# Row gradient of an 8192 x 8192 matrix: issuing each transfer midway through the one in front of it

**Chip, cores, metric.** One core of one Trainium2 chip. The metric is the device time of one execution in microseconds (us).

## What is computed

```python
def reference(x: np.ndarray) -> np.ndarray:      # x: 8192 x 8192, float32
    return np.gradient(x, axis=1)
```

Inside a row this is `(x[j+1] - x[j-1]) / 2`; at the two ends of a row it is the plain difference of the first two and of the last two elements. 268.4 MB are read and 268.4 MB written, with hardly any arithmetic.

## The kernel before

The matrix is cut into 32 sets. A set is a tile of 128 partitions with two rows each (64 KB on each partition, 8 MB in all). Three slots in SBUF are used in turn. GpSimd takes the differences at the row ends; VectorE makes the halved differences of both rows in one instruction and writes them, shifted by 64 elements, into the slot that it reads; the end values are then copied in, on VectorE or GpSimd, and the slot is stored. All transfers are issued by SyncE on one queue.

```python
    def load(i):
        b = slots[i % NB]
        ins = nc.sync.dma_start(out=b[:, SH : SH + W], in_=x_sets[i])
        loads.append(chain(i, ins, *([stores[i - NB]] if i >= NB else [])))
    ...
        for i in range(NB):                       # NB = 3
            load(i)
        for i in range(nsets):                    # nsets = 32
            ...                                   # GpSimd: ends
            last = i == nsets - 1
            nr = 1 if last else R                 # R = 2
            for r in range(0, R, nr):
                ...                               # VectorE: both rows at once; then the copy of the ends
                ins = nc.sync.dma_start(out=out_sets[i, :, ...], in_=b[:, ...])
                stores[i] = chain(i, ins, placed)
                if 2 <= i and not last:
                    tc.add_manual_dep(ins.ins, stores[i - 1].ins.name, landed, reason="behind a load that has begun")
            if 1 <= i and i - 1 + NB < nsets:
                load(i - 1 + NB)
```

`chain` only tells the framework which of the dependencies within a slot need a semaphore. The manual dependency makes a store wait, on the issuing side, until the store before it has landed. By then a load has begun. Store i and load i+2 so enter the queue together.

## Time and profile before

| | before |
|---|---|
| device time, first 3 runs | 1250.43 us median (1250.28 to 1250.81) |
| profiled run: span | 1247.7 us |
| DMA queue, share of 16 engines | 99.6% |
| VectorE busy | 554.8 us |
| one 8 MB transfer | 19.319 us between completions |

The last row comes from the DMA packet records, which lie in the trace beneath the page's totals: one record for each packet (here 64 KB, or 4 bytes for a completion), with its start and duration. The records don't name the engine, but each engine's packets follow one another end to end, so 16 chains can be followed. Everything below on "the last packet of a load" or on "spread" is worked out from them. Packet loss means the sum of what the packets took over 2.418 us for 64 KB, divided by 16: the time that it costs an engine on average.

The page's list of DMA issues (what goes where, how often, and the median from issue to landing) in the kernel before reads:

```profile
slot<-in_x_dram SPq DMA_DIRECT2D x32, 57.6
out_dram<-slot SPq DMA_DIRECT2D x31, 38.6
```

A store lands two transfers (38.6 us) after its issue, a load three (57.6 us): at each issue of the pair the queue holds nearly one whole transfer, then the store, then the load.

### The profile page before, as it was taken

The page shows a single profiled execution, that of the slowest core. Times are in us where ns is not written, and L with a number is a line of the kernel's source. Part 1 is how long each engine was busy: PE and PEld are TensorE (multiplying, and loading weights), DVE is VectorE, ACT ScalarE, POOL GpSimd, SP SyncE. Part 2 cuts the span into 40 slices and gives each one's busy share as a digit, 9 for nine tenths or more (in the row PEclk, how much of TensorE's full clock was granted, in tenths as well). Part 3 has the DMA queues.
Part 4 walks back from the last instruction along what each step waited for, and adds up shares of the span by engine and source line. Part 5 has one row for each costly group of instructions (what it writes and reads, how often), then busy time and mean ns, then how long its engine had stood idle before and what let it go on. Part 6 is the DMA issues. An engine that isn't in the chain of part 4 may idle for free.

```text
span 1247.7 us, 241 instructions
## 1 busy us (share of the span) xinstructions
DVE 554.8 (44%) x54; POOL 8.8 (1%) x48
## 2 busy tenths in 40 slices
DVE  2851455324553345533455334554335543355433
POOL 0000000000000000000000000000000000000000
DMA  9999999999999999999999999999999999999998
GB/s 403 437 437 424 424 429 435 435 435 431 431 437 433 427 431 433 429 435 437 437 437 435 427 431 437 427 433 437 437 437 437 435 431 429 435 433 437 431 433 357
DMA packets 9361, 536.88 MB, mean 430 GB/s; under 512 B 1040, under 2 KB 1040, under 8 KB 1040
## 3 DMA queue, kind: packets, MB, share of 16 engines
q1 hardware_dynamic: 9360, 536.88, 99.6%
q14 instruction: 1, 0.01, 0.0%
HBM read 268.44 MB, written 268.44 MB: 430 GB/s over the span
## 4 chain that ended last, share of the span: by engine, by line
another core or an unknown queue 68%; DVE 18%; DMA 8%; issue 3%; POOL 1%; POOLq 0%
DVE slot L82 18%; DMA slot<-in_x_dram 5%; DMA out_dram<-slot 3%; POOL ends L71 0%; POOL slot L93 0%; DVE slot L93 0%; POOLq L129 0%
## 5 line engine op out<-in xcount | busy, mean ns | idle before, releaser
L82 DVE CUSTOM_DVE_ANT_0 slot<-slot 128x16382 f32<-128x16382 f32 (+1 forms) x33 | 551.3, 16706 | 670.6 <-POOL ends L71 670.6
L71 POOL TENSOR_TENSOR ends<-slot 128x4 f32<-128x4 f32 x32 | 6.3, 198 | 991.5 <-DMA slot<-in_x_dram 991.5
L93 DVE COPY slot<-ends 128x4 f32<-128x4 f32 (+1 forms) x21 | 3.6, 171 | 0.7
L93 POOL COPY slot<-ends 128x4 f32<-128x4 f32 x12 | 2.3, 190 | 207.8 <-DVE slot L82 207.8
L118 POOL MEMSET const-bfloat16-1.0<- 128x1 bf16 x1 | 0.1, 102 | 0.0
L118 POOL MEMSET const-uint8-127<- 128x1 uint8 x1 | 0.1, 102 | 0.0
L118 POOL MEMSET const-float32-0.0<- 128x1 f32 x1 | 0.1, 98 | 0.2 <-issue 0.2
L118 POOL MEMSET const-float32-1.0<- 128x1 f32 x1 | 0.1, 98 | 0.0
## 6 DMA issues: line engine op xcount, KB each, us to landing
out_dram<-slot SPq DMA_DIRECT2D x2, 4096.0 KB, 20.2
slot<-in_x_dram SPq DMA_DIRECT2D x32, 57.6
out_dram<-slot SPq DMA_DIRECT2D x31, 38.6
```

Of the source, the lines that this page charges most:

```text
L71: ins = nc.gpsimd.tensor_sub(out=ends[:, i, :, :], in0=xin[:, :, 1 : m : m - 2], in1=xin[:, :, 0 : m - 1 : m - 2],)
L82: ins = nc.vector._custom_dve(dve_ops.TENSOR_TENSOR_REDUCE_SUB_MAX, out=b[:, c0:c1], in0=b[:, SH + c0 + 1 : SH + c1 + 1], in1=b[:, SH + c0 ...
L93: ins = placer.tensor_copy(out=res[:, :, 0 : m : m - 1], in_=ends[:, i, r : r + nr, :])
L118: nc = _bacc.Bacc("TRN2", target_bir_lowering=False, num_devices=1)
```

## The change

Its intent is to issue each transfer about midway through the one in front of it, and to take the moment for that from VectorE: an instruction for one row takes half a transfer's time, so its end is a clock. The first row of a set, which starts when the load has landed, gives the issue of the next load; the second row, which is made to wait until the store in front has landed, gives the issue of the set's own store. The end copies go to ScalarE, and at the start two loads are issued instead of three.

```diff
+    def follow(ins, needed, reason):
+        tc.add_manual_dep(ins.ins, needed.ins.name, landed, reason=reason)
+
-    def load(i):
+    def load(i, after=None):
         ...
+        if after:
+            follow(ins, after, "half-way through the transfer in front")
 ...
-        for i in range(NB):
-            load(i)
+        load(0)
+        load(1)
         for i in range(nsets):
 ...
-            for r in range(0, R, nr):
-                c0, c1 = r * m + 1, (r + nr) * m - 1
+            for r in range(R):
+                c0, c1 = r * m + 1, (r + 1) * m - 1
                 ins = nc.vector._custom_dve(...)
-                halved = chain(i, ins, *at)
-                ...
-                if 2 <= i and not last:
-                    tc.add_manual_dep(ins.ins, stores[i - 1].ins.name, landed, reason="behind a load that has begun")
-            if 1 <= i and i - 1 + NB < nsets:
-                load(i - 1 + NB)
+                at = chain(i, ins, at)
+                if r == 0:
+                    if i == 2:
+                        follow(ins, stores[0], "half-way through the second store")
+                    if i == 0 or 2 <= i < nsets - 1:
+                        load(2 if i == 0 else i + 1, after=at)
+                elif not last:
+                    follow(ins, loads[i + 1] if i < 2 else stores[i - 1], "half-way through the transfer in front")
+                if last:
+                    store(i, r, 1, place(nc.vector, i, r, 1, at))
+            if not last:
+                store(i, 0, R, place(nc.scalar, i, 0, R, at))
```

More of the change, by code (lines that the diff above doesn't have):

```diff
@@ L57, in chain, with store, place @@
         return ins
-    def load(i):
+    def follow(ins, needed, reason):
+        tc.add_manual_dep(ins.ins, needed.ins.name, landed, reason=reason)
+    def load(i, after=None):
         b = slots[i % NB]
         ins = nc.sync.dma_start(out=b[:, SH : SH + W], in_=x_sets[i])
+        if after:
+            follow(ins, after, "half-way through the transfer in front")
         loads.append(chain(i, ins, *([stores[i - NB]] if i >= NB else [])))
+    def store(i, r, nr, placed):
+        ins = nc.sync.dma_start(
+            out=out_sets[i, :, r * m : (r + nr) * m], in_=slots[i % NB][:, r * m : (r + nr) * m]
+        )
+        stores[i] = chain(i, ins, placed)
+    def place(engine, i, r, nr, halved):
+        res = slots[i % NB][:, r * m : (r + nr) * m].rearrange("p (t m) -> p t m", m=m)
+        to, of = res[:, :, 0 : m : m - 1], ends[:, i, r : r + nr, :]
+        ins = nc.scalar.copy(out=to, in_=of) if engine is nc.scalar else engine.tensor_copy(out=to, in_=of)
+        return chain(i, ins, halved)
     with tc.manual_schedule():
-        for i in range(NB):
-            load(i)
+        load(0)
+        load(1)
         for i in range(nsets):
             b = slots[i % NB]
+            last = i == nsets - 1
             xin = b[:, SH : SH + W].rearrange("p (t m) -> p t m", m=m)
@@ L75 @@
             )
-            at = [chain(i, ins, loads[i])]
-            last = i == nsets - 1
-            nr = 1 if last else R
-            for r in range(0, R, nr):
-                c0, c1 = r * m + 1, (r + nr) * m - 1
+            at = chain(i, ins, loads[i])
+            for r in range(R):
+                c0, c1 = r * m + 1, (r + 1) * m - 1
                 ins = nc.vector._custom_dve(
@@ L89 @@
                 )
-                halved = chain(i, ins, *at)
-                res = b[:, r * m : (r + nr) * m].rearrange("p (t m) -> p t m", m=m)
-                placer = nc.gpsimd if i % 5 in (1, 3) and not last else nc.vector
-                ins = placer.tensor_copy(out=res[:, :, 0 : m : m - 1], in_=ends[:, i, r : r + nr, :])
-                placed = chain(i, ins, halved)
-                ins = nc.sync.dma_start(
-                    out=out_sets[i, :, r * m : (r + nr) * m], in_=b[:, r * m : (r + nr) * m]
-                )
-                stores[i] = chain(i, ins, placed)
-                if 2 <= i and not last:
-                    tc.add_manual_dep(ins.ins, stores[i - 1].ins.name, landed, reason="behind a load that has begun")
-                at = [halved]
-            if 1 <= i and i - 1 + NB < nsets:
-                load(i - 1 + NB)
+                at = chain(i, ins, at)
[10 more added lines that the diff above has]
+                store(i, 0, R, place(nc.scalar, i, 0, R, at))
 _INS = ['x']
```

## The prediction

> **What bounds the kernel now.** I read the page's busy shares and DMA rows first, then the groups, then the DMA queue's own waits, then the time line around one step, and last the DMA packet records that the trace keeps under the page's totals.
>
> The page, parts 1 to 3: the only compute engine that does anything is VectorE at 44%. The DMA queue fills 99.6% of what 16 engines can give, and the GB/s row stands at 430 to 437 nearly everywhere. A kernel like this is bound by the DMA engines, and the question is only how much of their time isn't bytes at the full rate.
>
> ```profile
> span 1247.7 us, 241 instructions
> DVE 554.8 (44%) x54; POOL 8.8 (1%) x48
> ...
> GB/s 403 437 437 424 424 429 435 435 435 431 431 437 433 427 431 433 429 435 437 437 437 435 427 431 437 427 433 437 437 437 437 435 431 429 435 433 437 431 433 357
> ...
> q1 hardware_dynamic: 9360, 536.88, 99.6%
> ```
>
> The reader should notice that the dips (424, 427) lie in the first half, and that the first slice (403) and the last (357) are the ramp at both ends.
>
> The groups split by shape give the durations that the change re-uses. The one-row form already exists, in the last set:
>
> ```profile
> L82 DVE CUSTOM_DVE_ANT_0 slot<-slot 128x16382 f32<-128x16382 f32 x31 | 533.9, 17223 | 649.4 <-POOL ends L71 649.4
> L82 DVE CUSTOM_DVE_ANT_0 slot<-slot 128x8190 f32<-128x8190 f32 x2 | 17.4, 8686 | 21.2 <-POOL ends L71 21.2
> L71 POOL TENSOR_TENSOR ends<-slot 128x4 f32<-128x4 f32 x32 | 6.3, 198 | 991.5 <-DMA slot<-in_x_dram 991.5
> ```
>
> The queue's waits say that nearly all of them are a store that waits for the store before it, which is the manual dependency of this kernel. In the time line of one step, a store and the next load are issued together, 0.4 us apart, just after a store has landed, and the next pair follows 38.67 us later:
>
> ```profile
> SPq L95 <- DMA out_dram<-slot: 1082.2, 29, 38.8
> SPq L95 <- DVE slot L93: 74.7, 3, 38.2
> ```
>
> ```profile
> 918.42 0.33 SPq L95 DMA_DIRECT2D out_dram<-slot  x1
> 918.80 0.43 SPq L61 DMA_DIRECT2D slot<-in_x_dram  x1
> 937.75 0.20 POOL L71 TENSOR_TENSOR ends<-slot 128x4 f32<-128x4 f32 x1 [20.95 <-DMA slot<-in_x_dram]
> 937.98 17.22 DVE L82 CUSTOM_DVE_ANT_0 slot<-slot 128x16382 f32<-128x16382 f32 x1 [21.44 <-POOL ends L71]
> 955.24 0.17 DVE L93 COPY slot<-ends 128x4 f32<-128x4 f32 x1
> 957.09 0.33 SPq L95 DMA_DIRECT2D out_dram<-slot  x1
> ```
>
> At 918.42 the load in front has just begun (it lands at 937.75), so each pair goes into the queue a whole transfer, 19.3 us, ahead of need. Nothing starves.
>
> The packet records size what is left. A 64 KB packet takes 2.418 us when undisturbed. Packets of one engine chain end to end, and I followed the 16 chains (some 520 packets each). A transfer is 8 packets on each engine, and its completions come 19.319 us after those of the one in front; 64 of them (the two half stores count as one) make 64 x 19.319 = 1236.4 us. The first data packet starts at 1.75 us, and its first round is slowed by 0.7 us on average. The fastest engine thus ends at 1240.8 us. The slowest ends at 1246.46 us, and the span closes 1.2 us later. Those 5.6 us of spread are the only reserve. They come almost wholly from one place: the last packet of a load, when a store is next on the queue, takes 2.5 to 3.7 us in place of 2.42. From load to load or from store to load the step stays 19.32 us. The mean loss at that switch falls from 0.85 us (first store) through 0.45, 0.23, 0.30, 0.35 to nearly 0 after 800 us, while the spread of the 16 engines grows from 0.55 us to 5.64 us: once they no longer switch together, they no longer slow one another. That this is why it fades is my inference.
>
> **What the Trainium skill says.** "DMA: Bandwidth & Descriptors", section "Where 436 GB/s comes from", gives a port ceiling of 435.2 GB/s (16 ports). The trace agrees: 8,388,608 B in 19.319 us is 434.2 GB/s, so only the ends and the switches can be won. The same page, "Queues, rings and completion order": one queue has a ring on each of 16 engines, and each consumes its own in order. That fits the spread that grows and never resets, and means that a transfer issued too late would hit the fastest engine first. "SBUF — State Buffer", section "Who interferes with whom", holds that DMA doesn't contend with a compute engine. The trace agrees: while VectorE ran from 121.2 to 138.4 us the store under way kept its 19.319 us step. "ScalarE: Activation LUTs", section "What ACT_TABLE_LOAD costs", gives some 2.7 us for a table load. The kernel before runs nothing on ScalarE, so its trace shows none; one load at the start would be over long before the first copy is due near 50 us.
>
> **The change part by part.**
>
> 1. One row for each VectorE instruction: 31 x 17.22 us become 62 x 8.69 us, that is 538.8 in place of 533.9, plus 4.9 us of VectorE time. The 19 end copies of VectorE (171 ns) and the 12 of GpSimd (190 ns) move to 31 on ScalarE. VectorE stays at some 45% of the span and has slack in each step (17.4 of 38.6 us), so the path gains and loses nothing: 0 us.
>
> 2. The issue of a load: from "together with the store before it" to "after row 0 of the set that has just landed". Landing seen, subtraction, row: about 0.4 + 0.2 + 8.7 + 0.1 = 9.4 us after the previous load landed, the store in front being half done. Before the transfer in front ends, 19.3 - 9.4 = 9.9 us are left. The spread of up to 5.6 us takes its share of this for the fastest engine, and the first issue shows 1.0 us from issue (0.74) to first packet (1.75): 9.9 - 5.6 - 1.0 = 3.3 us of margin at the worst. No gap: 0 us.
>
> 3. The issue of a store: row 1 now waits for the store before it to land, then 0.8 us until seen (landed 100.49, issue 101.30 in the records before) + 8.7 + about 0.4 for the copy = 9.9 us into the load in front. Margin 9.4 - 5.6 - 1.0 = 2.8 us. 0 us.
>
> 4. The start: the third load is no longer issued at once, but after row 0 of set 0 at 22.9 + 8.7 = 31.6 us; the second load ends at 41.5. The first store comes after row 1, which waits for that load: about 41.9 + 8.7 + 0.4 = 51 us, with the third load ending at 61. Full either way: 0 us. The end is the same: load 31 lands near 1208, the two half stores are issued near 1217.5 and 1226.3, behind a store that ends near 1227.
>
> 5. What can be gained: the pair's issue no longer falls into the first two packets after a store. In the first 300 us I count 14 such packets, 60 to 360 ns too long each, 2.2 us in all over 16 engines; of the two slowest engines one has a single such packet (215 ns), the other none. A generous reading, that these also seed the later loss, makes it 1 us. The loss at the switch from load to store isn't an issue effect by its times: at 117 to 120 us nothing had been issued for 15 us. So I keep most of it: gain 0 to 2 us, and I take 1 us.
>
> Sum: 1250.4 - 1.0 = 1249.4 us.
>
> **The rivals.**
>
> First, the switch costs less because only one transfer, not two, is queued behind the load that ends. For it: the change's own intent, and that this loss is by far the largest term. Against it: the first store (0.85 us, the costliest) already had only other work behind it that was issued at about the same moment. If true, up to the whole spread goes: 1250.4 - 5.6 = 1244.8 us. The hard floor for this queue is near it.
>
> Second, the fastest engines run dry because the margin, 3 us, is eaten by a spread greater than before. Then they wait for an issue and the spread stops growing near 9 us. The slowest engine doesn't feel this, since it always has work, but switching together again might bring the loss back: some 1 to 3 us, up to 1253.
>
> Third, the change brings a stall at every step, because an issue is late for all engines. It would take 0.4 us at each of 64 transfers to make 2%, and issues come 9 us early. I see nothing in the profile for it.
>
> **Range and chances.** The point is 1249.4 us. Eight times in 10 it should lie between 1246.0 us (most of the switch loss gone) and 1252.0 us (spread somewhat worse). Faster by 2% would be below 1225.4 us, which is below the bytes at the full rate (1236.4 us), so 0.5% is left for it. Slower by 2% is above 1275.4 us and needs the third rival: 1%. Within 2%: 98.5%.
>
> **What would show it.** Queue share near 99.6% again; the load's time from issue to landing falling from 57.6 to about 38.6 - 9.4 = 29 us and the store's from 38.6 to about 29 us; 64 VectorE instructions of 8.69 us; issues on the time line some 19 us apart, each about midway between two landings. Landings still 38.64 us apart for each pair late in the run. In the packet records, the last packet of a load should still be slow at the first switches, and the spread should end between 4 and 7 us. If the spread ends below 3 us, the first rival holds and my step 5 is wrong. If gaps show between packets of the fastest engines, the second does. A time outside 1244 to 1254 would mean that I misread what sets the end.

## The result

| | before | after |
|---|---|---|
| runs | 6 | 6 |
| median, us | 1250.36 (1249.16 to 1250.81) | 1249.68 (1248.69 to 1250.33) |
| profiled run, span, us | 1247.7 | 1248.6 |

The ratio is 0.9995 with a 95% interval of 0.9982 to 1.0008: no difference that these runs could show. The profiled run of the changed kernel was its slowest, that of the kernel before one of its faster ones, so the two spans stand the wrong way round; that is chance.

The profile of the changed kernel, first its page (span, busy shares, the queue):

```profile
span 1248.6 us, 307 instructions
DVE 556.3 (45%) x66; ACT 7.4 (1%) x32; POOL 6.6 (1%) x36
...
q1 hardware_dynamic: 9360, 536.88, 99.5%
```

The groups, costliest first (busy us, mean ns of one, then idle time before them and what ended it):

```profile
L100 DVE CUSTOM_DVE_ANT_0 slot<-slot 128x8190 f32<-128x8190 f32 x64 | 556.1, 8690 | 670.5 <-POOL ends L91 341.7
L80 ACT COPY slot<-ends 128x4 f32<-128x4 f32 x31 | 6.1, 197 | 1190.5 <-DVE slot L100 1190.5
...
L80 ACT ACT_TABLE_LOAD x1 | 1.3, 1283 | 0.7 <-PEq L134 0.7
```

64 instructions of one row stand in place of 31 of two rows and two of one; their busy time rises from 551.3 to 556.1 us, and it lies in idle time.

The DMA issues and the queue's own waits show that the change did what it set out to do. A transfer now lands 1.5 transfers after its issue (29.7 us), loads and stores alike, and the queue no longer waits for a landing but for ScalarE's copy and for VectorE's row:

```profile
slot<-in_x_dram SPq DMA_DIRECT2D x32, 29.7
out_dram<-slot SPq DMA_DIRECT2D x31, 29.6
```

```profile
SPq L72 <- ACT slot L80: 591.7, 31, 19.9
SPq L66 <- DVE slot L100: 572.0, 30, 30.0
```

And the time line of one step late in the run (start, duration, engine, line, operation):

```profile
899.86 0.20 POOL L91 TENSOR_TENSOR ends<-slot 128x4 f32<-128x4 f32 x1 [38.40 <-DMA slot<-in_x_dram]
900.09 8.69 DVE L100 CUSTOM_DVE_ANT_0 slot<-slot 128x8190 f32<-128x8190 f32 x1 [10.77 <-POOL ends L91]
908.81 0.34 SPq L66 DMA_DIRECT2D slot<-in_x_dram  x1
919.28 8.69 DVE L100 CUSTOM_DVE_ANT_0 slot<-slot 128x8190 f32<-128x8190 f32 x1 [10.50 <-DMA out_dram<-slot]
928.01 0.20 ACT L80 COPY slot<-ends 128x4 f32<-128x4 f32 x1 [38.45 <-DVE slot L100]
928.23 0.33 SPq L72 DMA_DIRECT2D out_dram<-slot  x1
938.55 0.20 POOL L91 TENSOR_TENSOR ends<-slot 128x4 f32<-128x4 f32 x1 [38.49 <-DMA slot<-in_x_dram]
```

The load is issued at 908.81 and the store at 928.23, 19.4 us apart; before, they left 0.4 us apart. Yet the distance from one load's landing to the next (899.86 to 938.55 as GpSimd sees it) is 38.69 us, as it was in the kernel before. A store is issued half a transfer later than before (29.6 us ahead of its landing in place of 38.6), a load nearly one and a half transfers later (29.7 us in place of 57.6), and the landings stayed where they were.

What the packet records say of both profiled runs:

```
                                            before   after
first data packet, us                         1.75    1.75
packet loss in all, mean engine, us           4.63    4.09
  of it at the first load-to-store switch     0.83    1.03
  of it after 50 us                           3.93    3.45
fastest / slowest engine's last packet ends  1240.8 / 1246.5   1240.4 / 1247.3
```

So the same three things make up the time in both: 1236.4 us of bytes at the full rate, 4 us of start and end, and the 7 to 8 us that the slowest engine loses, nearly all of it in the packets that end a load when a store follows.

### The profile page after: what moved, and what is told of

The parts are those of the page before. It is cut to its first block, busy times and chain, and to the rows that moved or that the text cites. A ratio compares the mean times of both kernels' runs of the same rounds, so it can differ in the third digit from the quotient of the medians.

```text
span 1248.6 us, 307 instructions
## 1 busy us (share of the span) xinstructions
DVE 556.3 (45%) x66; ACT 7.4 (1%) x32; POOL 6.6 (1%) x36
## 3 DMA queue, kind: packets, MB, share of 16 engines
q1 hardware_dynamic: 9360, 536.88, 99.5%
## 4 chain that ended last, share of the span: by engine, by line
DMA 73%; DVE 22%; issue 3%; POOL 0%; SPq 0%; POOLq 0%; ACT 0%; DVEq 0%
DMA slot<-in_x_dram 70%; DVE slot L100 22%; DMA out_dram<-slot 2%; POOL ends L91 0%; SPq L66 0%; DVE slot L80 0%; POOLq L145 0%; ACT slot L80 0%; DVEq L100 0%
## 5 line engine op out<-in xcount | busy, mean ns | idle before, releaser
L100 DVE CUSTOM_DVE_ANT_0 slot<-slot 128x8190 f32<-128x8190 f32 x64 | 556.1, 8690 | 670.5 <-POOL ends L91 341.7
L80 ACT COPY slot<-ends 128x4 f32<-128x4 f32 x31 | 6.1, 197 | 1190.5 <-DVE slot L100 1190.5
L80 ACT ACT_TABLE_LOAD x1 | 1.3, 1283 | 0.7 <-PEq L134 0.7
## 6 DMA issues: line engine op xcount, KB each, us to landing
slot<-in_x_dram SPq DMA_DIRECT2D x32, 29.7
out_dram<-slot SPq DMA_DIRECT2D x31, 29.6
```

Of the source, the lines that this page charges most:

```text
L80: ins = nc.scalar.copy(out=to, in_=of) if engine is nc.scalar else engine.tensor_copy(out=to, in_=of)
L100: ins = nc.vector._custom_dve(dve_ops.TENSOR_TENSOR_REDUCE_SUB_MAX, out=b[:, c0:c1], in0=b[:, SH + c0 + 1 : SH + c1 + 1], in1=b[:, SH + c0 ...
```

## The experiments

There are two questions. The first is whether the time really doesn't depend on when a transfer is issued, or whether two effects of the change cancel. My theory: only an empty queue costs; rivals: the row-wise instructions cost and the issue times gain, or the other way round. The second is what makes the loss at the switch from load to store, the only reserve there is, and why it fades in the run. My theory (an inference in the prediction): engines that switch together slow one another, and the loss stops as they spread. Rivals: it fades with the age of the run; it depends on issue times.

All twelve kernels gave correct results. The table has the times; ratios are against the kernel before in the same rounds on the same chip.

```
run                            median (range), us              ratio [95% interval]
e1 row-wise alone              1250.71 (1249.07 to 1251.55)    1.0003 [0.9989, 1.0017]
e2 no manual wait              1249.49 (1248.92 to 1251.72)    0.9998 [0.9984, 1.0012]
e3 issue 7.6 us later          1323.54 (1321.26 to 1327.53)    1.0591 [1.0572, 1.0610]
e4 first load cut in six       1269.17 (1268.18 to 1270.59)    1.0153 [1.0139, 1.0167]
e5 stagger, half a packet      1255.01 (1252.45 to 1257.14)    1.0031 [1.0018, 1.0045]
e6 stagger, two extra loads    1257.47 (1255.46 to 1257.90)    1.0052 [1.0040, 1.0064]
e7 transfers of 4 MB           1256.77 (1255.81 to 1273.37)    1.0081 [1.0036, 1.0126]
e8 issue 3.9 us later          1250.67 (1249.07 to 1257.08)    1.0011 [0.9990, 1.0032]
e9 stagger, one packet         1255.02 (1253.13 to 1256.73)    1.0040 [1.0026, 1.0054]
e10 stagger, 1.5 packets       1256.09 (1255.25 to 1257.21)    1.0048 [1.0035, 1.0061]
e11 the changed kernel again   1250.35 (1249.83 to 1250.82)    1.0001 [0.9988, 1.0013]
e12 stagger, 11 rows           1254.64 (1253.43 to 1255.29)    1.0032 [1.0018, 1.0046]
```

### e1: the row-wise part alone

The kernel before, with a second VectorE instruction for the second row, and everything else as it was:

```diff
-                c0, c1 = r * m + 1, (r + nr) * m - 1
+                c0, c1 = r * m + 1, (r + 1) * m - 1
                 ...
                 halved = chain(i, ins, *at)
+                if nr == R:
+                    c0, c1 = m + 1, R * m - 1
+                    ins = nc.vector._custom_dve(...)
+                    halved = chain(i, ins, halved)
```

> One part of the change alone: the kernel before with one VectorE instruction for each row, its issue times untouched (the second row only follows the first). Theory (only the 16 engines' own time counts): 62 instructions of 8.69 us on VectorE, a store ready some 0.3 us later in each step, which no transfer sees; 1249 to 1251 us, spread of the engines at the end 4 to 7 us. Rival (row-wise work delays the queue): over 1252 us and a queue share under 99%.

Measured: 1250.71 us, ratio 1.0003. The packet loss is 3.8 us. Its groups are the two halves:

```profile
L82 DVE CUSTOM_DVE_ANT_0 slot<-slot 128x8190 f32<-128x8190 f32 x33 | 286.8, 8690 | 663.8 <-POOL ends L71 663.8
L93 DVE CUSTOM_DVE_ANT_0 slot<-slot 128x8190 f32<-128x8190 f32 x31 | 269.4, 8691 | 1.1
```

This part of the change costs nothing by itself, so it doesn't hide a gain of the other part.

### e2: a store issued when its data is ready

```diff
-                if 2 <= i and not last:
-                    tc.add_manual_dep(ins.ins, stores[i - 1].ins.name, landed, reason="behind a load that has begun")
```

> The kernel before without its manual wait of a store for the store before it. A store is then issued when its data is ready, some 2 us before the store in front has landed instead of 0.8 us after. Theory (issue times don't matter while something is queued): 1249 to 1251.5 us, loss at the switch from load to store as before (4 to 5 us in all on the mean engine). Rival (the loss depends on when the pair is issued): the loss changes by more than 1.5 us, to either side.

Measured: 1249.49 us, ratio 0.9998; packet loss 4.05 us. The time line shows that the store has moved as meant:

```profile
567.68 0.17 DVE L93 COPY slot<-ends 128x4 f32<-128x4 f32 x1
567.88 0.33 SPq L95 DMA_DIRECT2D out_dram<-slot  x1
569.46 0.34 SPq L61 DMA_DIRECT2D slot<-in_x_dram  x1
```

The store follows its copy at once and stands 1.6 us ahead of the load, which must still wait for the slot. Neither the time nor the loss answers to this.

### e3 and e8: later and later issues

The changed kernel with a maximum over N elements of the row just written, on VectorE, after each row; its result is used by nothing, only its end is waited for. N is 7168 in e3 and 3584 in e8.

```diff
                 at = chain(i, ins, at)
+                if not last:
+                    ins = nc.vector.tensor_reduce(
+                        out=spent[:, :], in_=b[:, r * m + 1 : r * m + 1 + DELAY], axis=mybir.AxisListType.X, op=mybir.AluOpType.max
+                    )
+                    at = chain(i, ins, at)
```

> The changed kernel with a 7168-element maximum of VectorE (about 7.5 us, result unused) after each row, so that every issue comes about 17 us after the landing in front, 1 us before the slowest engine would run dry. A fast engine that is over about 1 us ahead has then nothing to do and waits, so the 16 engines are held together. Theory (the loss at a load-to-store switch comes from many engines switching together, and fades only as they spread): spread held below 2 us, the loss stays at 0.2 to 0.6 us at each of 31 switches instead of fading, and the time goes to 1254 to 1266 us. Rival A (the loss fades with the age of the run, whatever the spread): 1249 to 1252 us. Rival B (fewer transfers queued behind a load make the switch cheaper): under 1248 us.

> The changed kernel with a 3584-element maximum after each row (about 3.8 us by the 7.62 us that 7168 elements took), so that each issue comes some 13.5 us after the landing in front instead of 9.7 us, about 5.8 us before the slowest engine needs it; less some 1 us until the first packet. Theory (only a dry queue matters): the fastest engines are caught when the spread passes some 4.5 us, the slowest is not, 1249 to 1253 us. Rival B (issue time moves the loss): over 1254 us or under 1247 us.

Measured for e8: 1250.67 us, no difference, with VectorE 64% busy. The extra instruction takes 3.9 us, so each issue comes that much later:

```profile
L112 DVE TENSOR_REDUCE spent<-slot 128x1 f32<-128x3584 f32 x62 | 240.9, 3886 | 9.5 <-DMA out_dram<-slot 7.5
```

The spread of the engines stays at 3.1 to 3.9 us from 370 us on where the changed kernel lets it grow to 6.9. I had expected fast engines to be caught by an empty queue once the spread passed 4.5 us; it never did, and the longest gap between two packets of an engine is 0.36 us. So running dry isn't what held the spread, and what did isn't found. The mean engine loses more (6.5 us instead of 4.1), and still the slowest ends at 1247.0 us, where the changed kernel's ends at 1247.3. It is the slowest engine that sets the time.

Measured for e3: 1323.54 us, well beyond the 1254 to 1266 us that I expected. Its page shows that the queue ran dry, which the theory hadn't foreseen for all engines:

```profile
DVE 1025.8 (78%) x128; ACT 7.4 (1%) x32; POOL 12.3 (1%) x36
...
q1 hardware_dynamic: 9360, 536.88, 97.6%
```

```profile
L112 DVE TENSOR_REDUCE spent<-slot 128x1 f32<-128x7168 f32 x62 | 472.4, 7620 | 2.1
```

The packet records divide what was lost, 75 us more than in the kernel before on the mean engine (whose packet loss was 4.6 us there). Idle gaps between packets: 30 us more, nearly all ahead of loads. First packets after a gap of over 0.2 us: 11 us too long in all. The last packets of loads: 31 us, which is 1.0 us at each of 30 switches (the expectations count 31; the first two loads are followed by a load). Other slow packets, most of them early in a load: 7 us. In the kernel before the 30 switches cost 3.7 us together. So the landing of the slowest engine, delayed by the switch, delays the issue and empties the queue for many engines; the switch then costs 1.0 us again, up to the end of the run (26 of the 49 us of packet loss lie after 640 us). That rules out that the loss fades with age alone. It doesn't show that standing together is what keeps the loss: at a load's landing the engines are 0.6 to 3.4 us apart, not below 2 us as expected, and the gaps and restarts are new as well. More than half of the extra time is slow packets and not an empty queue, so "only an empty queue costs" was too narrow. It also shows where the slack of the changed kernel ends: 3.9 us later is free, 7.6 us later costs 6%.

### e4: the first load cut so that the engines carry unequal shares

```diff
-        for i in range(NB):
-            load(i)
+        for t in range(R):
+            for p0, p1 in ((0, 5), (5, 16), (16, P)):
+                c = t * m
+                ins = nc.sync.dma_start(out=slots[0][p0:p1, SH + c : SH + c + m], in_=x_sets[0, p0:p1, c : c + m])
+                pieces.append(chain(0, ins))
+        ...
+        for i in range(1, NB):
+            load(i)
```

> The kernel before with its first load cut into six: each of the two rows as 5, 11 and 112 partitions. By the Trainium skill, page DMA: Bandwidth & Descriptors, section Why a DMA increments its semaphore by 16 and not by 1, a transfer of 5 partitions runs on the lowest 5 engines, of 11 on the lowest 11, of 112 on all 16. The engines then carry 18, 16 and 14 rows of 32 KB in this load in place of 16, and 5, 6 and 5 of them stand about 2.4 us apart from the start; bytes are the same. Theory (switching together costs): the loss at the switches falls from 4.6 us on the mean engine to below 2.5 us; the slowest engine carries 2.4 us more by design and ends at 1243 to 1245.5 in place of 1246.5; time 1247 to 1249.5 us. Rival A (age of the run): the loss stays, on top of the 2.4 us: 1251 to 1254 us. Rival B (issue times): the same, 1251 to 1254 us.

Measured: 1269.17 us, 1.5% slower, against 1247 to 1249.5 us expected. Both halves of that are instructive. Stretches of the run, first e4 and then the kernel before (from:to, length, VectorE busy, GpSimd busy, clock, DMA share, GB/s):

```profile
0.00:20.00 20.00, 0.00 (x0) 0.20 (x4) 1.00 0.92 211
20.00:50.00 30.00, 0.00 (x0) 0.07 (x1) 1.00 1.01 209
50.00:100.00 50.00, 46.09 (x4) 0.72 (x4) 1.00 1.01 439
```

```profile
0.00:20.00 20.00, 0.00 (x0) 0.20 (x4) 1.00 1.00 419
20.00:50.00 30.00, 25.19 (x3) 0.40 (x2) 1.00 0.97 419
50.00:100.00 50.00, 26.82 (x3) 0.39 (x2) 1.00 1.00 425
```

In the first 50 us of e4 the engines are busy and move half the bytes: the 32 KB packets of the cut load take up to 4.5 us (2.4 us in the median; the half stores at the end of the kernel before take 1.21), and the first 64 KB packets behind them up to 4.9 us instead of 2.42. This alone costs 24.5 us. Why, no run isolates. The number of completions, 2 x (5 + 11 + 16) = 64 for the cut load, fits what the expectation quotes from the skill's page on the engines used, so a wrong number of engines isn't the reason; e12 below has one more hint. From 50 us on the packet loss is 0.18 us in the whole rest of the run, where the kernel before loses 3.93. The engines stand in groups of 5, 6 and 5, at 0 to 0.5, 2.0 to 2.5 and 3.9 to 5.3 us, from the first switch to the last. So the loss can be absent from the beginning, which again speaks against age, and also against any part of it being a fixed price of the switch. It also speaks against another rival, the addresses: the same bytes go through the same 30 switches here as in the kernel before.

### e5 and e6: a stagger by extra loads

To have the stagger without the bad start, 8 engines load some rows twice, ahead of all else (into slot 2, which the third load then overwrites after a wait that costs nothing).

```diff
+    def stagger(e, cols):
+        ins = nc.sync.dma_start(out=slots[2][0 : 4 * e : 4, SH : SH + cols], in_=x_sets[2, 0 : 4 * e : 4, 0:cols])
+        extra.append(chain(2, ins))
...
+        for e in (8,):            # e6: (4, 8), with 48 KB rows
+            stagger(e, W)
```

> The run with a first load cut into 5, 11 and 112 partitions showed no loss at all at the switches once three groups of engines stood 2 us apart, but paid 24 us for its start[...]. Here the stagger is made without that: ahead of all loads of the kernel before, 8 engines load one 64 KB row each (partitions 0, 4 ... 28[...]; 0.5 MB that is thrown away). They stand 2.42 us behind the other 8 from the start. Theory (loss from switching together): the loss at the switches falls from 4.6 us to 1 to 3 us on the mean engine (groups of 8 may still slow each other); slowest engine at 1240.8 + 2.4 + 0.5 to 2 = 1243.7 to 1245.2 us; time 1247.5 to 1249.5 us, although 0.1% more bytes are moved. Rival A (the loss fades with age or with the addresses): loss unchanged, slowest engine 2.4 us later than before, 1251.5 to 1254 us.

> As the run before it, with two extra loads of 48 KB rows: on 4 engines, then on 8. Engines stand in three groups 1.8 us apart (4 engines 3.6 us behind, 4 engines 1.8 us, 8 engines in front). Theory: loss at the switches below 2 us on the mean engine, slowest at 1240.8 + 3.6 + 0 to 1 = 1244.4 to 1245.4 us; time 1247.8 to 1249.5 us. Rival A: 1252.5 to 1255 us.

Measured: 1255.01 and 1257.47 us, both slower, and both theories' numbers missed. In e5 the packets show two groups of 8 engines 1.2 us apart: the issue of the extra load held the others' first packet back from 2.3 to 3.5 us, so the stagger was half a packet. At the first switch all 16 engines lost 1.75 us (0.83 in the kernel before); in all they lost 8.9 us. e6 is a flawed experiment: its two extra loads overlap, so the second waited for the first, 5 us of start were lost, and two groups of 8 remained. Its first switch cost 1.67 us, but after 50 us it lost only 4.6 us in all where e5 lost 8.5, although its groups too stood about half a packet apart or less.

### e7: more switches

```diff
-    R = 2
-    NB = 3
+    R = 1
+    NB = 6
```

> The kernel before with one row in each transfer (4 MB) and six buffers, so 58 switches from load to store in place of 31. Theory (the loss stops by itself once the engines have spread by 4 to 6 us): it is reached in half the time but is not more; loss 4 to 6 us on the mean engine, spread 4 to 7 us, 1249 to 1252.5 us. Rival (a fixed price for each switch, 4.6 us for 31): loss near 8.6 us, 1254 us or more.

Measured: 1256.77 us (three runs of 1255.8 to 1257.4, and the profiled one at 1273.4). This one decides nothing. Its loss up to 520 us is 5.0 us against 3.8 us in the kernel before, with twice as many switches, which leans to the theory. After that the spread passes 7.5 us, a transfer is only 9.7 us long, fast engines run dry, and the loss rises to 1 us in each 40 us. At the end, where no loads are left, each store waits for the one before it to land with nothing in front: in the profiled run three of the last landings are 11.1, 11.2 and 11.1 us apart instead of 9.7. I should have taken the manual wait away in the tail.

### e9 and e10: the stagger made exact

The extra load goes between the first and the second load, so that nothing is held back.

```diff
-        for i in range(NB):
-            load(i)
+        load(0)
+        for p, cols in ((0, W),):             # e10: ((0, W), (1, W // 2))
+            stagger(p, cols)                  # partitions p, p + 4 ... p + 28
+        for i in range(1, NB):
+            load(i)
```

> In the two stagger runs before, the groups of 8 engines ended up only 1.2 us apart (the extra load's issue also held back the other group), half the 2.42 us of a packet, and each switch cost more than without a stagger (8.9 us in all instead of 4.6). In the run with the first load cut the groups stood one packet apart and the switches cost nothing. Here the extra 64 KB row of 8 engines is queued between the first and the second load, so that the 8 stand exactly one packet, 2.42 us, behind the other 8, and start with them. Theory (the loss is made while many engines are in the last packet of a load at the same time): loss at the switches below 2.5 us on the mean engine, slowest engine at 1240.8 + 2.4 + 0.5 to 2 = 1243.7 to 1245.2, time 1247.3 to 1249.5 us. Rival A (fades with age only): loss 4 to 6 us, 1251.5 to 1254 us. Rival C (any stagger by halves of the engines makes it worse): loss over 7 us, 1254 us or more.

> The same with 64 KB and then 32 KB more on these 8 engines, 3.63 us or one and a half packets. Theory: the two groups never are in their last packet together; loss as in the run before or less (0.7 us of the start and 0 to 2 us), slowest engine at 1240.8 + 3.6 + 0 to 1.5 = 1244.4 to 1246, time 1248 to 1250 us. If what counts is the phase of the packets rather than their overlap, the loss is again over 7 us and the time 1255 us or more.

Measured: 1255.02 and 1256.09 us; packet loss 9.1 and 9.3 us. The theory of the prediction, that distance between the engines stops the loss, falls here. At one packet's distance the halves aren't in their last packets together, and at a switch near 235 us the 8 in front still lose about 0.9 us and the 8 behind, a packet later, 1.1 us. Other switches of this run cost nothing (0.01 us in the two after the first), with the same distance between the groups. Rival C, "any stagger by halves makes it worse", has the right numbers but explains nothing.

### e11: the changed kernel again

> The changed kernel once more, for the sign of a difference that six runs left open (0.7 us between the medians, interval of the ratio 0.9982 to 1.0008). Theory (issue times don't matter): ratio 0.999 to 1.001, medians within 1 us. Rival (a small gain from the issue between the switches): ratio 0.9985 or less with an interval below 1.

Measured: 1250.35 us against 1249.89 us for the kernel before, ratio 1.0001. The sign of the small difference turned round; it was noise. The profiled run has a packet loss of 3.6 us and its engines end between 1240.3 and 1246.8 us.

### e12: meant to make three groups

As e9, with 11 partitions (0, 4 ... 40) in the extra load:

```diff
-        ins = nc.sync.dma_start(out=slots[2][p : 32 : 4, SH : SH + cols], in_=x_sets[2, p : 32 : 4, 0:cols])
+        ins = nc.sync.dma_start(out=slots[2][p : 44 : 4, SH : SH + cols], in_=x_sets[2, p : 44 : 4, 0:cols])
```

> Two halves of 8 engines apart by a half, one and one and a half packets all lost about 9 us at the switches instead of 4.6: the theory that distance alone stops the loss has fallen. The run with the first load cut (groups of 5, 6 and 5, one packet apart) lost 0.2 us after its bad start. Here one extra load of 11 rows of 64 KB (partitions 0, 4 ... 40) is queued between the first two loads of the kernel before; [...]I expect engines in groups of about 6, 5 and 5, at 4.8, 2.4 and 0 us. Theory now (what counts is how many engines are in the last packet of a load together: 8 still lose, 5 or 6 don't): loss after 50 us below 1 us on the mean engine (3.9 in the kernel before), slowest engine at 1240.8 + 4.8 + 0 to 0.5 = 1245.6 to 1246.1 us, time 1248.5 to 1250.5 us. Rival (the cut load was quiet for another reason, and any stagger by an extra load costs more): loss after 50 us 6 to 9 us, 1254 to 1258 us.

Measured: 1254.64 us, packet loss after 50 us 3.1 us: between the two numbers. But the run isn't the one that was meant. While the extra load ran, one packet of each of the 16 engines took 4.0 to 4.7 us, on the five that had no row of it too; with the packet behind it that is 2.4 us lost on the mean engine. The 8 rows of e9 slowed no packet so. And the completion packets show two groups, not three: from the second load on 5 engines stand in front and 11 stand 2.2 us behind them.

The first switch cost 0.02 us and the next ones up to 160 us 0.09, as in e4 (0.03 and 0.02) and unlike the kernel before (0.83 and 0.67). So a group of 11 passed the first switches free, and the theory that 8 engines together lose and 5 or 6 don't isn't borne out either. Later the loss came back: from 160 us on the five in front fell back until, near 350 us, they were only 0.5 us ahead. At the end five engines ended between 1249.2 and 1252.1 us, the other eleven between 1244.0 and 1244.6. What keeps the loss away for a whole run in e4, and not here, isn't found. With one more row on 11 engines (2.4 us) and 2.4 us lost at the start, the version had little to win, and it doesn't win.

The losses below come from one profile of each run. In the five profiles of kernels that leave the engines to themselves (before, changed, e1, e2, e11) the loss after 50 us lies between 3.0 and 3.9 us.

```
packet loss, us      first switch   after 50 us   engines
before                   0.83          3.93       16 together, spreading by themselves
e3                       1.24         48.54       0.6 to 3.4 us apart, many run dry before a load
e4                       0.03          0.18       5, 6, 5, one packet apart
e5                       1.75          8.49       8, 8, half a packet apart
e6                       1.67          4.63       8, 8, half a packet apart or less
e8                       1.12          6.03       16 together, spreading to 3.9 us
e9                       1.16          8.43       8, 8, one packet apart
e10                      0.97          8.71       8, 8, one and a half packets apart
e12                      0.02          3.07       5, 11, one packet apart at first
```

No run beat both kernels.

## Why the prediction was right, point by point

1. *The bound.* Right. The queue's share went from 99.6% to 99.5%, and no change of issue time moved the landings as long as something was queued: e2 (1.6 us earlier), the change itself (stores half a transfer later, loads one and a half) and e8 (3.9 us later still) all lie within 0.11% of the kernel before. e3 shows the other side of the edge. Two readings under this head were off; the first rival's 1244.8 us rests on the second, the forecast on neither. Two of the three dips to 427 GB/s lie in the second half of the run (slices 23 and 26). And 1.75 + 0.7 + 1236.4 us make 1238.9 us, not 1240.8 (1239.1 for the mean engine, which starts at 2.0): the fastest engine too loses nearly 2 us at the switches, so the reserve was some 7.4 us on the slowest engine and not 5.6.
2. *VectorE's and ScalarE's part, 0 us.* Right: the row instructions' busy time rose by 4.8 us as worked out, and e1 puts its cost at nothing.
3. *The margins.* Right in kind. Load issues come 9.3 us after the slowest landing (899.49 in the packet records, 908.81 the issue), store issues 9.4 us (918.80 to 928.23) where I had 9.9: the wait for the landing took 0.5 us until VectorE ran, not 0.8, and the copy 0.2.
4. *Start and end, 0 us.* Right: third load issued at 31.6 us, first store at 51.0, first packet at 1.75 us in both.
5. *A gain of 1 us from issues that no longer fall behind a store.* Not shown. The slow packets at the head of a load did go, from 14 in the first 300 us to 2, but the medians differ by 0.7 us one way and 0.5 us the other. This term should have been 0: those packets were 2.2 us over 16 engines, and mostly not on the slowest one. That the point of 1249.4 us lies 0.3 us from the median is so in part luck.
6. *First rival (fewer queued transfers make the switch cheaper).* Wrong, as held: the first switch cost 0.83 us before and 1.03 after.
7. *Second rival (fast engines run dry, and the slowest doesn't feel it).* It doesn't happen in the changed kernel, whose spread reached 6.9 us, near the end of the range of 4 to 7 us. e8 was to provoke it and didn't (longest gap 0.36 us); in e3 many engines ran dry at once, and the time felt that. The case of a few fast engines alone stays untested.
8. *The inference on why the loss fades.* This is the step that didn't hold as put. Being apart isn't enough: two halves one packet apart lost twice as much as engines that were left alone. Starting again from an empty queue keeps the loss (e3), groups of 5, 6 and 5 escape it for a whole run (e4), and groups of 5 and 11 at the first switches only (e12). So neither the distance nor the number that switch together decides by itself. Whether engines slow one another at a switch at all, and in which arrangements, stays open; nothing in the time of the change depended on it.

## What to carry to other kernels

When one queue is 99% busy and every issue already comes well before the queue is empty, as here, don't expect a gain from moving issues; the slack (here between 4 and 8 us) is worth knowing only to stay inside it. Look at the slowest DMA engine rather than at the mean, because all landings wait for it. And before cutting a transfer into odd numbers of partitions, check the GB/s of that stretch: half the rate over 50 us costs more than any reordering here could give.

## What the Trainium skill lacked or had wrong

- "DMA: Bandwidth & Descriptors" has nothing on a price for turning from loads to stores on one queue. Here the last packet of a load took up to 3.7 us instead of 2.42 when a store followed, 0.83 us on the mean engine at the first switch, 3.7 us over the 30 switches of the run, and 1.0 us at each of 30 in e3. From store to load the step stayed at 19.32 us.
- The same page tells how the number of engines follows from the partitions, and advises using all 16, but not that such a transfer can slow every engine. Transfers of 5, 11 and 112 partitions at the start of e4 ran at 209 to 211 GB/s in place of 419, the one of 112 on all 16 engines; one of 11 rows in e12 slowed a packet on each of the 16 to 4.0 to 4.7 us, one of 8 rows in e9 none. No run here shows why.
- "HBM Reference", section "Specifications (TRN2)", gives about 425 GB/s for a core that streams alone. Alternating 8 MB loads and stores ran at 434.2 GB/s for one transfer (19.319 us) and 430 GB/s over the whole span, close to the port ceiling of 435.2 GB/s that the DMA page gives.
- "ScalarE: Activation LUTs", section "What ACT_TABLE_LOAD costs", gives 1283 ns for the table load itself, and the trace has 1283 ns; the drain that the page adds to it isn't visible in the trace of this kernel.
